# Two mixers of a hybrid encoder trunk: TensorE's queue in the order the code is written, in place of the scheduler's order

## The chip, the cores and the metric

One core of a Trainium2 chip runs the whole kernel. The engines named here are TensorE (PE, matmuls; PEld is its weight load), VectorE (DVE), ScalarE (ACT), GpSimd (POOL) and SyncE (SP, which issues DMAs). Each takes its own instructions one after the other and waits on semaphores for the others. The metric is the device time of one execution in microseconds (us), lower is better.

## What is computed

A two-layer encoder over 16 meta tokens and 512 tokens (T = 528), width 1024, 8 heads, float32. Layer 0 has mixer A, sparse attention: an indexer scores all keys, each query keeps its best 128, and attention runs over those. Layer 1 has mixer B, differential attention, two softmax maps per head with one subtracted from the other. A gated ConvFFN ends each layer.

```python
# mixer A, per block of 128 queries
score = jnp.einsum('bqh,bqhs->bqs', wib, jax.nn.relu(s))   # s: index queries x index keys
_, idx = lax.top_k(jnp.where(vis[None], score, NEG_INF), k_top)
logits = jnp.einsum('bqgrd,bqkgd->bqgrk', qg, ksel) * scale + bias
o = jnp.einsum('bqgrk,bqkgd->bqgrd', jax.nn.softmax(logits), vsel)
# mixer B, per block of 128 queries
lg = jnp.einsum('bqhd,bshd->bhqs', qb, kk) * scale + bias      # once with q1,k1 and once with q2,k2
a = attn_map(q1b, k1) - lam * attn_map(q2b, k2)
o = jnp.einsum('bqhs,bshd->bqhd', a, vb)
# every layer
h = h + mixer(rms_norm(h)); h = h + conv_ffn(rms_norm(h))
```

## The kernel before

The activations lie transposed (features on partitions, the 528 tokens along the free axis) and are cut in two halves of 272 and 256 tokens. A float32 product is made from three matmuls of rounded parts, `hi`x`hi`, `hi`x`lo` and `lo`x`hi`: `lin` (L306, in the helper `mm`) is such a projection, 8 slices of the contraction by 2 halves by 3, so 48 matmuls, for one block of 128 output features. Each block of weights is loaded by SP, rounded on ACT (`hi`, L168) and its rest taken on DVE or POOL (`lo`, L176).

`mixer_a` makes index keys and queries, the index scores (`is`, L875) and the top-k on DVE (rounds of L923 and L924 in `select`), the queries of the first group (`queries_a`, its four blocks followed by the sums of squares `stq`, L681), and then attends (`attend_a`): scores `sa` (L1024, three matmuls per piece), minimum and mask on DVE (L1026), exponent on ACT, transposes `pt` (L1128), rounding `ph` on ACT and `pl` on DVE, product with the values `pv` (L1119).

`mixer_b` goes through four pairs of heads, p = 0 to 3. `project(p)` makes keys, queries (`stq` again at L681, after the squares of L1531 on ACT) and values by 6 `lin`. `attend_b` goes through 16 units, `UNITS`: pair, head of the pair, half of the queries. In a unit a chunk of keys is a step: the scores `sb` of the next unit (L1670 and L1671) with their DVE reduction (L1673) and the exponent (L1679), the `pv` (L1745) of the chunk before, then the transposes `pt` (L1759) of this chunk, `ph` (L1763, ACT) and `pl` (L1764, DVE). The two maps are combined on DVE (L1689 to L1692).

The Python code runs once and records the instructions. The order in which it records them is made by a clock that counts estimated TensorE time: `fill(us)` lets the `filler` (the projections of the next pair, or the output projection) record `lin` matmuls until so much time has been counted, `defer` records something once the clock has passed. The filler gives nothing where it is blocked:

```python
for m in range(2):
    while self.unit < 4 * (p - 1) + 2 * m and p > 0:
        yield False
    yield from self.lin(x, lambda u, m=m: evac_q(u, m))
...
for t in range(len(chunks) + 1):
    next(nxt, None)            # scores of the next unit
    self.fill(0.5 * G)
    # pv of the chunk before, pt, ph and pl of this one
    self.fill(0.5 * G)
```

A scheduler then makes each engine's queue from the recorded instructions: by its own model of time it takes, for each engine, what is ready, and goes by the recorded order among those. In a region `tc.manual_schedule(engines=...)` the named engines keep the recorded order. The main part of `ffn` (the pairs of `up_pair`) is such a region of PE, DVE and ACT in both kernels; the mixers have none before. All of PSUM's small tiles (`sa`, `sb`, `pt`, `pv`, `stq`) share four buffers, tag "one".

Of the kernel before, what the change touches and what calls it, by code (L numbers as in the profile page):

```python
# [1876 lines left out]
@with_exitstack  # L1877
def trunk_kernel(ctx, tc, aps, out):
    t = Trunk(ctx, tc, aps, out)
    t.setup()  # L1880
    t.mixer_a()
    t.ffn(0)
    t.mixer_b()
    t.ffn(1)


# [53 lines left out]
```

## Time and profile before

| | |
|---|---|
| three timed runs | 1365.03, 1370.22, 1372.44 us; median 1370.22 |
| profiled execution, its own time | 1369.62 us |
| span from its first to its last instruction | 1367.8 us |
| PE busy in the span | 1284.9 us, 94% |
| DVE, ACT, POOL busy | 1032.4, 716.7, 343.3 us |

Mixer A runs from the start to about 290 us of the span, the first `ffn` to 655, mixer B to 985, the second `ffn` to the end. Matmuls are pipelined, so that a matmul shown with 0.28 us begins 0.12 us after the one before: the distance between starts is what one costs the queue. PEclk is the share of the full TensorE clock that was granted.

### The profile page before, as it was taken

Reading aid. Unit: us, or ns where it says so; the run is one execution under the profiler, and the core shown is the slowest. Engines: PE = TensorE matmul, PEld = TensorE weight load, DVE = VectorE, ACT = ScalarE, POOL = GpSimd, SP = SyncE. Lnnn points to the kernel's source line nnn. Section 1 sums busy time; section 2 is a strip of 40 time slices with the busy share of each in tenths; the row PEclk is TensorE's granted clock in tenths of the full one; section 3 lists DMA queues with packets and bytes.
Section 4 is the critical chain, followed back from the end, with each engine's and each line's share of the span. In section 5 each row is a group of like instructions: output and inputs, shape, how many; then the busy total and the mean of one; then the engine's idle time right before and its main releaser. Section 6 shows DMA issues by size and latency. Waiting matters only on the chain.

```text
span 1367.8 us, 25126 instructions
## 1 busy us (share of the span) xinstructions
PE 1284.9 (94%) x9688; PEld 1233.5 (90%) x9688; DVE 1032.4 (75%) x2030; ACT 716.7 (52%) x1426; POOL 343.3 (25%) x398
## 2 busy tenths in 40 slices
PE   5999889897999999989899999989897999999998
PEld 4999889897999999989799999989787999999986
DVE  6499977687888888776657777776787888888873
ACT  4453555564555555554435555655464555555541
POOL 3513543410111111103444644444510111111100
PEclk9999999989999999999899989999999999999999
DMA  7312222121455445533222222212221454554432
GB/s 236 107 61 76 88 83 80 62 78 62 117 133 146 127 125 130 132 79 106 92 63 89 68 67 63 71 48 73 67 88 62 120 146 129 127 148 127 118 90 93
DMA packets 58519, 136.03 MB, mean 99 GB/s; under 512 B 7216, under 2 KB 16736, under 8 KB 58400
## 3 DMA queue, kind: packets, MB, share of 16 engines
q1 hardware_dynamic: 48432, 114.57, 25.7%
q0 software_dynamic: 9968, 19.87, 9.5%
q8 instruction: 76, 1.25, 0.4%
q14 instruction: 43, 0.35, 0.1%
HBM read 112.46 MB, written 4.91 MB: 86 GB/s over the span
## 4 chain that ended last, share of the span: by engine, by line
PE 80%; DVE 11%; ACT 4%; issue 2%; POOL 1%; DMA 1%; SPq 0%; ACTq 0%; DVEq 0%; POOLq 0%
PE lin L306 22%; PE dn L1374 18%; PE g L1240 17%; PE v L1240 12%; DVE c L1331 2%; PE pv L1745 1%; PE stq L681 1%; PE pv L1119 1%; PE linh L306 1%; DVE lo L176 1%; DVE xl L630 1%; ACT hi L168 1%; PE sa L1024 1%; PE stk L671 1%; PE sb L1671 1%
## 5 line engine op out<-in xcount | busy, mean ns | idle before, releaser
L306 PE MATMUL lin<-xh,hi 128*128 128x256 f32 (+3 forms) x928 | 272.2, 298 | 13.6 <-DVE ht L547 7.1
L306 PE MATMUL lin<-xl,hi 128*128 128x256 f32 (+3 forms) x928 | 272.3, 295 | 2.1 <-DVE xl L630 1.8
L306 PE MATMUL lin<-xh,lo 128*128 128x256 f32 (+3 forms) x928 | 271.8, 294 | 0.0
L168 ACT CAST hi<-raw 128x512 fp32r<-128x512 f32 (+3 forms) x225 | 178.8, 824 | 90.9 <-PE lin L306 47.6
L176 DVE TENSOR_TENSOR lo<-raw,hi 128x1024 fp32r<-128x1024 f32 (+3 forms) x196 | 179.1, 929 | 55.1 <-ACT hi L168 52.1
L1410 POOL DMA_DIRECT2D ht<-y x64 | 55.8, 872 | 569.3 <-ACT y L1409 560.6
L306 PEld LDWEIGHTS lin<-xh,hi 128*128 128x128 f32 (+1 forms) x928 | 179.7, 196 | 17.1 <-ACT xh L656 8.6
L306 PEld LDWEIGHTS lin<-xl,hi 128*128 128x128 f32 (+1 forms) x928 | 181.2, 195 | 3.8 <-DVE xl L630 3.2
L306 PEld LDWEIGHTS lin<-xh,lo 128*128 128x128 f32 (+1 forms) x928 | 181.1, 195 | 0.0
L1240 PE MATMUL g<-xh,hi 128*128 128x264 f32 (+1 forms) x480 | 137.3, 286 | 11.3 <-DVE c L1331 6.6
L1374 PE MATMUL dn<-al,hi 128*128 128x256 f32 (+2 forms) x528 | 143.0, 321 | 0.0
L1374 PE MATMUL dn<-ah,lo 128*128 128x256 f32 (+2 forms) x528 | 142.2, 320 | 0.0
L1374 PE MATMUL dn<-ah,hi 128*128 128x256 f32 (+2 forms) x528 | 142.2, 321 | 0.0
L1240 PE MATMUL v<-Th,lo 128*128 128x264 f32 (+1 forms) x480 | 136.9, 285 | 0.0
L1240 PE MATMUL v<-Tl,hi 128*128 128x264 f32 (+1 forms) x480 | 136.5, 284 | 0.0
L1240 PE MATMUL v<-Th,hi 128*128 128x264 f32 (+1 forms) x480 | 136.3, 284 | 0.0
L1240 PE MATMUL g<-xh,lo 128*128 128x264 f32 (+1 forms) x480 | 136.0, 283 | 0.0
L1240 PE MATMUL g<-xl,hi 128*128 128x264 f32 (+1 forms) x480 | 135.7, 283 | 0.0
L1240 PEld LDWEIGHTS g<-xh,hi 128*128 128x128 f32 x480 | 90.4, 188 | 15.4 <-ACT hi L168 7.7
L176 DVE TENSOR_TENSOR lo<-S,hi 128x1024 fp32r<-128x1024 f32 x80 | 97.2, 1216 | 0.0
L1374 PEld LDWEIGHTS dn<-ah,lo 128*128 128x128 f32 x528 | 89.0, 188 | 7.4
L1374 PEld LDWEIGHTS dn<-ah,hi 128*128 128x128 f32 x528 | 88.8, 188 | 5.7 <-ACT hi L168 1.1
(301 smaller groups left out, 3290.7 us busy)
## 6 DMA issues: line engine op xcount, KB each, us to landing
raw<-w_up SPq DMA_DIRECT2D x88, 512.0 KB, 3.7
raw<-w_down SPq DMA_DIRECT2D x64, 256.0 KB, 3.5
ht<-y POOLq DMA_DIRECT2D x32, 264.0 KB, 3.9
raw<-w_in SPq DMA_DIRECT2D x16, 512.0 KB, 3.6
raw<-w_kv SPq DMA_DIRECT2D x16, 512.0 KB, 3.6
ht<-y POOLq DMA_DIRECT2D x32, 256.0 KB, 3.8
raw<-w_down SPq DMA_DIRECT2D x16, 384.0 KB, 3.2
nb<-nbias SPq DMA_DIRECT2D x16, 264.0 KB, 2.7
```

The lines of the kernel that those rows point to most:

```text
L168: nc.scalar.copy(hi[:, :n, :m], src)
L176: eng.tensor_tensor(lt[:, :n, :m], src, hi[:, :n, :m].bitcast(F32), op=OP.subtract)
L306: i = self.nc.tensor.matmul(o, w[wi][:, kw + k, :m], x[s][xi][:, kx + k, c0:HN[s]], start=(first and p == 0), stop=(last and p == 2))
L630: i = eng.tensor_tensor(xl[:, m, o:o + n], xfs[m][:, :n], xh[:, m, o:o + n].bitcast(F32), op=OP.subtract)
L671: self.nc.tensor.matmul(st[:88, 2 * c:2 * c + 2], sq[:, 88 * c:88 * (c + 1)], rhs, start=True, stop=True)
L681: self.nc.tensor.matmul(st[:, c:c + 2], sq[:, c0:c0 + 128], rhs, start=True, stop=True)
L1024: nc.tensor.matmul(s, q[:, c0:c0 + 128], k[:, k0:k1], start=(p == 0), stop=(p == 2))
L1119: nc.tensor.matmul(pv[:, :4 * nq], v[:, c, :], pp[:, :, :nq], start=(ci == 0 and p == 0), stop=(ci == nch - 1 and p == 2))
L1240: nc.tensor.matmul(out, w[wi][:, wk + k, :], xs[xi][:, xk + k, c0:c0 + N], start=(first and k == 0 and p == 0), stop=(k == 3 and p == 2), ...
L1331: nc.vector.scalar_tensor_tensor(t[:, z:n], u[:, off + t0 + z - d:off + T - d], w, t[:, z:n], op0=OP.mult, op1=OP.add)
L1374: nc.tensor.matmul(part(t, c0, c1, o), w[wi][:, k, :], acts[f][ai][:, c0:c1], start=(first and p == 0), stop=(last and p == 2))
L1410: nc.gpsimd.dma_start(self.h[m][:, t0:T], y[:, :n], accum_op=OP.add)
```

## The change

`mixer_a` and `mixer_b` are put in regions in which PE keeps the recorded order. No instruction is added, removed or altered, and the queues of the other engines are still made by the scheduler, which now has a given PE order to go by.

```diff
     t.setup()
-    t.mixer_a()
+    with tc.manual_schedule(engines={mybir.EngineType.PE}):
+        t.mixer_a()
     t.ffn(0)
-    t.mixer_b()
+    with tc.manual_schedule(engines={mybir.EngineType.PE}):
+        t.mixer_b()
     t.ffn(1)
```

PE's queue where mixer A's attention begins, behind the last `stq` of the first group's queries. Before:

```order
L681 MATMUL stq<-ones,sq 128x2 x5
L1024 MATMUL sa<-kh,qh 128x272
L1024 MATMUL sa<-kl,qh 128x272
L1024 MATMUL sa<-kh,ql 128x272
L1024 MATMUL sa<-kh,qh 128x256
L1024 MATMUL sa<-kl,qh 128x256
L1024 MATMUL sa<-kh,ql 128x256
L1024 MATMUL sa<-kh,qh 128x272
L1024 MATMUL sa<-kl,qh 128x272
L1024 MATMUL sa<-kh,ql 128x272
```

And of the change:

```order
L681 MATMUL stq<-ones,sq 128x2 x5
L1024 MATMUL sa<-kh,qh 128x272
L1024 MATMUL sa<-kl,qh 128x272
L1024 MATMUL sa<-kh,ql 128x272
L1024 MATMUL sa<-kh,qh 128x256
L1024 MATMUL sa<-kl,qh 128x256
L1024 MATMUL sa<-kh,ql 128x256
```

Before, one more piece of scores follows, then 13 `lin`, the fourth piece, and 60 `lin` ahead of the fifth; of the change 12 `lin`, the third and fourth piece, and 12 `lin` ahead of the fifth. So between the `stq` and the fifth piece there stand 12 matmuls of scores in both, with 73 `lin` before and 24 of the change.

PE's queue in mixer B at the first `stq` of pair 1, in the last steps of pair 0's first unit (names as above; `few` is a tile of the meta queries). Before:

```order
L681 MATMUL stq<-ind,sq 128x2 x5
L306 MATMUL lin<-xh_8145,lo 128x272
L306 MATMUL lin<-xh_7979,hi 128x256
L306 MATMUL lin<-xl_7980,hi 128x256
L306 MATMUL lin<-xh_7979,lo 128x256
L306 MATMUL lin<-xh_8145,hi 128x272
L306 MATMUL lin<-xl_8146,hi 128x272
L1745 MATMUL pv<-ph,vh 128x256
L306 MATMUL lin<-xh_8145,lo 128x272
```

And of the change:

```order
L681 MATMUL stq<-ind,sq 128x2 x5
L1745 MATMUL pv<-ph,vh 128x128
L1745 MATMUL pv<-pl,vh 128x128
L1745 MATMUL pv<-ph,vl 128x128
L1670 MATMUL sb<-kst,qst 128x272
L1671 MATMUL sb<-kl_8072,qst 128x272
L1670 MATMUL sb<-kst,qst 128x256
L1671 MATMUL sb<-kl_8072,qst 128x256
L1759 MATMUL pt<-ident,xs 128x128
L1759 MATMUL pt<-ident,few_8699 128x128
L1759 MATMUL pt<-ident,xs 128x128
```

Of the change no `lin` stands from the `stq` on for 33 rows, up to the scores `sb` that follow the fourth `pv` behind it; in the order before 82 `lin` matmuls stand among the same instructions.

DVE's queue of the change at that place; the row of `rq` reads the `stq` above, the third `pl` belongs to the first `pv` of 128x272 that follows:

```order
L176 TENSOR_TENSOR lo<-raw,hi 128x1024
L1532 SCALAR_TENSOR_TENSOR qst<-lin,gs,qst 64x528
L1764 TENSOR_TENSOR pl<-pt,ph 128x128
L1532 SCALAR_TENSOR_TENSOR qst<-lin,gs,qst 64x528
L688 TENSOR_SCALAR rq<-stq 128x8
L689 TENSOR_SCALAR rq<-stq 16x2
L1673 ISA xx,sm<-sb,tm,rq 128x272
L1673 ISA sm 128x1
L1673 ISA xx,sm<-sb,tm,sm,rq 128x256
L1673 ISA sm 128x1
L1764 TENSOR_TENSOR pl<-pt,ph 128x272
```

There follow the reductions of one more 272, one 256 and two 400 wide pieces, a `pl` of 256, one combination of 528 columns and a `pl` of 128. Before, these rows stand in nearly the same sequence (the second `qst` behind the rows of `rq`), with the keys of pair 1 (L1556, L1563) and another `lo` between the reductions; of the change those have moved behind them.

## Rows read from the trace of the kernel before

**Rows 1.** The page's head: span, then PE's busy time and the granted clock in 40 slices.

```profile
span 1367.8 us, 25126 instructions
PE 1284.9 (94%) x9688; PEld 1233.5 (90%) x9688; DVE 1032.4 (75%) x2030; ACT 716.7 (52%) x1426; POOL 343.3 (25%) x398
PEclk9999999989999999999899989999999999999999
```

**Rows 2.** Busy time by stretch: mixer A, first ffn, mixer B, second ffn.

```profile
core 0: us, PE busy (x) PEld busy (x) DVE busy (x) ACT busy (x) POOL busy (x), PEclk, DMA share, GB/s
10.00:290.00 280.00, 259.54 (x1939) 246.10 (x1940) 216.77 (x553) 138.63 (x313) 106.99 (x112) 0.97 0.30 92
290.00:655.00 365.00, 351.36 (x2846) 348.41 (x2844) 289.16 (x409) 198.70 (x348) 42.68 (x42) 1.00 0.43 113
655.00:985.00 330.00, 311.41 (x2444) 303.59 (x2444) 228.00 (x634) 176.91 (x437) 154.67 (x187) 0.94 0.23 69
```

**Rows 3.** PE's waits, mixer A then B: engine line waited for, us, times, longest.

```profile
PE pv L1119 <- ACT ph L1132: 3.0, 5, 0.7
PE pt L1128 <- POOL xx L1042: 1.8, 3, 1.0
...
PE pv L1745 <- DVE pl L1764: 3.0, 2, 1.7
PE Rk L703 <- POOL ex L698: 2.4, 2, 2.0
```

**Rows 4.** The chain that ended last, a `lin` of 48 matmuls at full clock: start, us.

```profile
113.80 5.96 PE lin L306 x48
```

**Rows 5.** Timeline of ACT before the last `stq` of mixer A: start, us.

```profile
121.99 1.05 ACT L168 CAST hi<-raw 128x1024 fp32r<-128x1024 f32 x1 [4.82 <-PE lin L306]
123.54 0.60 ACT L945 ACTIVATE sq<-lin 128x528 f32<-128x528 f32 x1
```

**Rows 6.** Timelines at mixer A's first scores: PE, DVE, POOL.

```profile
126.56 1.17 PE L681 MATMUL stq<-ones,sq 128*128 128x2 f32 x10
138.05 0.28 PE L1024 MATMUL sa<-kh,qh 128*128 128x272 f32 x1
131.02 0.19 DVE L478 TENSOR_TENSOR rq<-rq 128x40 f32<-128x40 f32 x1
136.50 0.49 DVE L1026 CUSTOM_DVE_ANT_0 xx<-sa,tm,rq 128x272 f32<-128x272 f32 x1
131.24 2.40 POOL L176 TENSOR_TENSOR lo<-raw,hi 128x1024 fp32r<-128x1024 f32 x1 [5.70 <-ACT hi L168]
133.60 3.09 POOL L1003 TENSOR_TENSOR tm<-tm,W 128x528 f32<-128x528 f32 x2
```

**Rows 7.** `lin` alone in mixer B, from pair 1's `stq` on: busy us (count).

```profile
747.20:764.90 17.70, 12.02 (x82) 10.83 (x82) 1.00 0.28 88
```

**Rows 8.** DVE groups, 700 to 950 us: shapes, count, busy us, mean ns, idle before.

```profile
L176 DVE TENSOR_TENSOR lo<-raw,hi 128x1024 fp32r<-128x1024 f32 x17 | 22.0, 1296 | 8.3 <-ACT hi L168 8.2
L1764 DVE TENSOR_TENSOR pl<-pt,ph 128x256 fp32r<-128x256 f32 x39 | 15.9, 413 | 4.6 <-ACT ph L1763 4.4
L1673 DVE CUSTOM_DVE_ANT_0 xx<-sb,tm,rq 128x400 f32<-128x400 f32 x16 | 10.0, 629 | 2.6 <-PE sb L1671 1.9 <-POOL tm L1639 0.5
L1532 DVE SCALAR_TENSOR_TENSOR qst<-lin,gs,qst 64x528 fp32r<-64x528 f32 x12 | 9.2, 766 | 2.7 <-ACT sq L1531 2.4
L1673 DVE CUSTOM_DVE_ANT_0 xx<-sb,tm,sm 128x256 f32<-128x256 f32 x16 | 8.7, 541 | 6.1 <-PE sb L1671 5.3
L1673 DVE CUSTOM_DVE_ANT_0 xx<-sb,tm,rq 128x272 f32<-128x272 f32 x16 | 8.0, 498 | 7.6 <-PE sb L1671 7.5
L1692 DVE SCALAR_TENSOR_TENSOR xx<-xx,sm 128x528 f32<-128x528 f32 x8 | 6.4, 800 | 0.1
```

**Rows 9.** ACT groups, 700 to 950 us, columns as in rows 8.

```profile
L168 ACT CAST hi<-raw 128x1024 fp32r<-128x1024 f32 x17 | 17.7, 1040 | 6.6 <-PE lin L306 6.6
L1763 ACT CAST ph<-pt 128x256 fp32r<-128x256 f32 x39 | 13.8, 362 | 5.8 <-PE pt L1759 5.1 <-PE pv L1745 0.4
```

**Rows 10.** Mixer B where the clock falls: two stretches as in rows 2, PE's timeline between.

```profile
800.00:805.00 5.00, 4.64 (x39) 4.36 (x37) 3.99 (x13) 3.74 (x10) 3.31 (x3) 1.00 0.07 15
805.00:810.00 5.00, 4.07 (x23) 4.10 (x24) 3.04 (x8) 1.89 (x5) 1.54 (x1) 0.54 0.33 107
805.93 1.89 PE L671 MATMUL stk<-ind,sq 128*88 128x2 f32 x12 [1.17 <-DVE ss L1792]
```

## The prediction

> **What bounds the kernel now.** I read the page's head first: PE is busy 94% of the span, the next engine, DVE, 75% [rows 1]. So PE decides, and a change of its order can gain what PE waits, or lose what it will wait. By stretch [rows 2], PE is busy 259.5 of 280 us in mixer A and 311.4 of 330 in mixer B: 20.5 and 18.6 us idle. The two `ffn` keep their order. The granted clock is 0.97 in mixer A and 0.94 in mixer B against 1.00 in the first `ffn`; 0.06 of 330 us is 20 us that mixer B loses to the lower level, 0.03 of 280 us is 8 us in A. The waits of PE inside attention are short [rows 3]: in A 3.0 us at `pv` and 1.8 at `pt`, in B 3.0 us at `pv`, in 2 places, of 64 steps, and 2.4 at `Rk`. So the scheduler's order leaves little to gain there; most of the idle time in both mixers stands at the norms, where there is no other work in either order.
>
> **What the change does.** No instruction is added. What changes is which PE instruction stands behind which, so the cost is time in which the first of the queue isn't ready and a `lin` that could have run stands behind it. I counted, for every `pv`, how many `lin` stand ahead of it in either order. Before, more stand ahead at each: the scheduler runs projections early while attention is held up. This lead goes up and down: in mixer A 0 to 84, down to 14, 72, 37, 89, 57, 83, and 0 at the end; in mixer B 0 to 162, then 74, 108, 84, 150, 88, 107, 84, 118, 26, 48, 22, 96, and 0. Where it rises, the order before has cover that the change lacks; where it falls, the change has the `lin` that was used before. One `lin` matmul costs 5.96/48 = 0.124 us at full clock [rows 4]. The rises are 84+58+52+26 = 220 in A and 162+34+66+19+34+22+74 = 411 in B, together 631, or 78 us. That is the upper bound: it holds if attention goes on as slowly as before and all the cover was needed. It was not, since PE found the operands of `pv` waiting for it in almost every step. The lower bound is nothing, where an operand arrives within the cover that is left. So I work out the places where the recorded order has little or no cover.
>
> **Start of attention in A.** Between the last `stq` and the fifth piece of scores lies a chain that doesn't depend on `lin`: `stq` from 126.56 to 127.73, the roots done at 131.2, bias and mask on ACT and POOL, the reduction on DVE from 136.50 to 136.99, which frees a buffer for the fifth piece (it ran at 138.05, behind `lin`) [rows 6]. That is 9.3 us behind the `stq`. Before, 12 matmuls of scores and 73 `lin` filled it; of the change 12 and 24 do: 36 x 0.124 = 4.5 us. The wait is 4.8 us. From below, POOL's `lo` of 2.40 us stands in the way of the mask [rows 6], and without it the wait is 2.4. I take 4.8, since the top-k on DVE and that `lo` stay. The `stq` itself stands right behind the projection whose squares it sums. Its squares end at 123.54+0.60 = 124.14, the rounding set off by that projection's end starts at 121.99 [rows 5]: 2.2 us, which before lay behind `lin`. From there on the recorded order spreads the `lin` more evenly over A's attention than the scheduler did, which had used them up, and I give back 3 us of the 4.8 us of waits at `pv` and `pt` [rows 3]. Mixer A: 4.8+2.2-3 = +4.
>
> **Stretches without `lin` in B.** Four times, once a pair, the filler is blocked at the queries of the next pair, and the recorded order has attention alone: 33 rows behind pair 1's first `stq`, 25 and 25 in the next two pairs and 81 in the last, `pv` among them. At the first of them, PE's own work from the `stq` to the fourth `pv` is 29 matmuls and the `stq`: 29 x 0.124 + 1.17 = 4.8 us, with an `stq` as in mixer A [rows 4, 6]. DVE must in that time do what the order shows, in its order: `lo` 1.30, two `qst` 1.53, two `pl` 0.83, two reductions of 272, two of 256 and two of 400 columns 1.00+1.08+1.26, a combination 0.80 [rows 8]: 7.8 us, without two `pl` and six small instructions. It can't begin with `lo` before ACT has made `hi`, 1.04 us [rows 9]. So the stretch lasts at least 7.8+1.0 = 8.8 us, and PE waits 4.0; with the small instructions nearer 5. I take 4.5. Before, at the same instructions, PE did 82 `lin` in 17.7 us, 12.0 us busy [rows 7], and DVE and ACT had that much more time. The stretches of pairs 2 and 3 begin with the same `lo` and `qst` and have fewer matmuls, the last has more but also more DVE work; I price each at 4.5, 4, 4 and 4.5, together 17. From both sides: 0 to 2 us each if DVE comes there with its queue empty and ACT's rounding is early; 10 us for the first if it costs the whole of the 82 `lin` (82 x 0.124 = 10.2).
>
> **The other steps of B.** About 48 steps have 12 `lin` between `pt` and `pv`, 1.5 us, against ACT's `ph` 0.36 and DVE's `pl` 0.41 [rows 8, 9]: hidden, as long as DVE takes the `pl` within 0.7 us. It has other work for 228 of 330 us [rows 2], and a `lo` or a 400-column reduction ahead costs more than that. I put 0.06 us on each, an estimate, +3, and take nothing off for B's present waits, which are mostly the norms'. Other engines get new orders too; what they shift counts only through these waits. The DMA share is 0.23 to 0.30 in the mixers [rows 2], so weights are not late.
>
> **The clock.** [...] I take the sum of the two as nothing, and 8 us either way as the bound (20 us lost in B now, 40% of it).
>
> The sum, against the profiled execution's own 1369.62 us (0.6 under the median of the three): 1369.6 + 4 + 17 + 3 = 1393.6, so **1394 us**, 1.7% slower.
>
> **The rivals.**
> - Faster: DVE and ACT keep up. It is decided at the step between `pt` and `pv`: if the chain is done within the 1.5 us of cover everywhere, and DVE arrives at the four stretches with nothing queued, the waits of rows 3 go (10.2 us) and only the lower bounds stand against it: 2.4 in A, nothing in B: 1369.6-10.2+2.4 = 1362. For it: PE waited at `pv` in 2 places of B only. Against it: that was with the cover of 20 us in front. Chance 0.14.
> - No change to be told (within 0.5%, 6.9 us, which is about what a measurement of this kernel can tell): the waits at the stretches are those that now stand elsewhere, some 5 us net: 1370 to 1376. For it: the same matmuls, and the idle time at the norms stays. Chance 0.14.
> - Much slower: the cover is needed for most of its length, because four PSUM buffers and DVE's queue hold each other up in the fixed order (a score waits for the reduction of the piece before, and all else of PE behind it), and PE's gaps bring the clock down more often. Two thirds of the 78 us: 1369.6+52 = 1422, and with 8 us of lower clock 1430. Against it: DVE has a third of its time free in B. Chance 0.14. [...]
> - My forecast, 1380 to 1412: 0.58.
>
> **How the numbers follow.** Slower by over 0.5%: 0.58+0.14 = 0.72; same 0.14; faster 0.14. The range leaves out half of the faster case and half of the much slower one, and a little of the forecast's ends: 1364 to 1424.
>
> **What would show it.** Right: PE's busy time in the mixers nearly the same as in rows 2, the idle time near 40 us in B and 25 in A; new waits of PE at `pv` on `pl`, of `sb` on the reduction, of the first `sa` on DVE; the two `ffn` unchanged to 1 us. Wrong in the first step: no wait of 3 us or more ahead of the fifth piece of scores in A. Wrong in the second: the four stretches pass with under 2 us of waits each, which would mean that DVE had done `lo` and `qst` before. Wrong altogether: DVE's queue, made for a PE that stands still, is so much better that attention goes faster than before.

## The result: slower by 8.5%, and the profile after

The changed kernel takes 1487.4 us (median of 4, 1483.5 to 1490.3), the kernel before 1371.3 us on the same chip: a ratio of 1.085, 95% interval 1.080 to 1.090. The forecast was 1394, its range ended at 1424. The direction was right; the loss is 116 us where 24 were worked out.

The head of the page of the changed kernel, to be laid beside [rows 1]:

```profile
span 1482.6 us, 25160 instructions
PE 1340.4 (90%) x9688; PEld 1277.1 (86%) x9688; DVE 1032.4 (70%) x2030; ACT 722.8 (49%) x1426; POOL 335.3 (23%) x398
PEclk9999979999999999998987879878999999999999
```

The span is 114.8 us longer with the same number of matmuls. PE's busy time has risen by 55.5 us, and what it isn't busy by 59.3 (1482.6 - 1340.4 = 142.2, before 1367.8 - 1284.9 = 82.9). So the loss has two halves, waiting and busy time that has become longer. The clock's row tells why the second: in mixer B eight of the ten slices from the 19th on hold a 7 or an 8. Busy time by stretch (us of the stretch, busy us and count of each engine, granted clock), with the three stretches of [rows 2], shifted:

```profile
core 0: us, PE busy (x) PEld busy (x) DVE busy (x) ACT busy (x) POOL busy (x), PEclk, DMA share, GB/s
10.00:317.50 307.50, 273.46 (x1938) 255.27 (x1939) 223.39 (x553) 140.67 (x313) 106.31 (x112) 0.93 0.28 84
317.50:681.50 364.00, 350.00 (x2847) 347.05 (x2846) 290.16 (x409) 199.17 (x348) 42.42 (x42) 1.00 0.43 114
681.50:1100.00 418.50, 353.77 (x2444) 339.18 (x2444) 220.73 (x633) 179.12 (x434) 149.08 (x188) 0.85 0.18 55
```

Mixer B is 88.5 us longer, mixer A 27.5, the `ffn` is not. DVE and ACT do nearly the same work in mixer B as before and are busy for 221 and 179 of 418.5 us: neither is the bound by its work. The granted clock of mixer B is 0.85 against 0.94: 0.15 x 418.5 = 63 us lost to the lower level, before 20.

PE's waits in mixer A, then in mixer B (engine, line, waited for: us in total, times, longest), to be laid beside [rows 3]:

```profile
PE pt L1128 <- POOL xx L1042: 6.3, 3, 4.9
PE pv L1119 <- DVE pl L1133: 4.9, 11, 1.1
PE sa L1024 <- DVE sm L1026: 3.7, 1, 3.7
PE stq L681 <- ACT sq L945: 3.5, 2, 2.1
...
PE stq L681 <- ACT sq L1531: 23.1, 8, 4.1
PE sb L1670 <- DVE sm L1673: 10.8, 16, 2.2
PE vt L713 <- ACT vf L1571: 8.1, 7, 2.2
PE stq L681 <- ACT sqo L1788: 4.3, 2, 2.1
PE pv L1745 <- DVE pl L1764: 2.6, 4, 1.1
```

In mixer B the most is waited at `stq`, for ACT's square of the projection that has just ended, then at `sb` for the reduction that frees a score's buffer, and at `vt` (transposes of the values) for ACT's copy of them. The next view, PE's timeline at the first `stq` of pair 1 (start, us; in brackets the wait and who ended it), is one of the four stretches that the prediction priced:

```profile
781.60 0.27 PE L1759 MATMUL pt<-ident,xx 128*128 128x128 f32 x1
785.54 2.29 PE L681 MATMUL stq<-ind,sq 128*128 128x2 f32 x10 [3.67 <-ACT sq L1531]
787.69 0.45 PE L1745 MATMUL pv<-ph,vh 128*128 128x128 f32 x1
...
788.71 0.43 PE L1671 MATMUL sb<-kl,qst 128*128 128x272 f32 x1
788.93 0.41 PE L1670 MATMUL sb<-kst,qst 128*128 128x256 f32 x1
...
795.03 0.38 PE L1745 MATMUL pv<-pl,vh 128*128 128x256 f32 x1 [1.07 <-DVE pl L1764]
...
796.06 0.33 PE L1745 MATMUL pv<-ph,vh 128*128 128x128 f32 x1 [0.41 <-ACT ph L1763]
...
797.24 0.43 PE L306 MATMUL lin<-xh,hi 128*128 128x272 f32 x1
```

PE stands for 3.67 us ahead of the `stq`. Behind it the sums take 2.29 us where [rows 6] have 1.17 for the same ten, and two neighbours of 256 to 272 columns are 0.22 us apart (788.71 and 788.93) where [rows 4] give 0.124. The stretches say the same, with the granted clock as the third column from the end:

```profile
783.50:793.70 10.20, 8.16 (x34) 7.78 (x34) 4.81 (x15) 3.98 (x9) 3.09 (x3) 0.50 0.17 52
793.70:797.20 3.50, 2.02 (x12) 1.42 (x12) 3.33 (x12) 2.00 (x6) 1.33 (x4) 0.99 0.49 134
797.20:800.60 3.40, 3.40 (x18) 3.40 (x16) 1.32 (x6) 1.54 (x6) 0.77 (x2) 0.50 0.17 47
```

Within the wait of 3.67 us a stretch of 10.2 us at a granted clock of 0.50 begins; the two waits of 1.07 and 0.41 are followed by another of 3.4 us. What held ACT's square up stands on the timelines of DVE and ACT (in the third row ACT's second copy `qst` has waited for DVE's first, which stood behind a weight's `lo`):

```profile
782.12 1.23 DVE L176 TENSOR_TENSOR lo<-raw,hi 128x1024 fp32r<-128x1024 f32 x1 [0.92 <-ACT hi L168]
783.37 0.76 DVE L1532 SCALAR_TENSOR_TENSOR qst<-lin,gs,qst 64x528 fp32r<-64x528 f32 x1
784.17 0.70 ACT L1529 ACTIVATE qst<-lin,gs 64x528 fp32r<-64x528 f32 x1 [1.34 <-DVE qst L1532]
784.88 0.61 ACT L1531 ACTIVATE sq<-lin 128x528 f32<-128x528 f32 x1
```

The table below is worked out from the traces in the same way for every run that follows, but for e6 and e16, which are told in their sections. Mixer A is the time up to the first `T` of the first `ffn`, mixer B that from the end of its last `dn` to the first `T` of the second (`T` is an `ffn`'s first product, `dn` its last). "Waits" is what of it no TensorE instruction covers, "low" the sum of the clock's records at half of full speed. A mixer's length is taken as its work at full clock, its waits, and half of its low time; so reckoned, mixer B's work is 308.1 us before and 306.9 changed, and mixer A's 250.1 and 252.0.

| run | time, us | ratio to before (95%) | A: us, waits, low | B: us, waits, low |
|---|---|---|---|---|
| before | 1371.3 | | 288.4, 29.8, 17 | 351.1, 22.5, 41 |
| changed | 1487.4 | 1.085 (1.080 to 1.090) | 315.9, 43.4, 41 | 439.8, 67.9, 130 |
| e1 region on A alone | 1395.0 | 1.019 (1.017 to 1.022) | 316.5, 43.2, 44 | 350.4, 19.7, 48 |
| e2 region on B alone | 1453.1 | 1.063 (1.059 to 1.067) | 286.3, 28.2, 14 | 439.4, 67.2, 130 |
| e3 sums later | 1476.4 | 1.079 (1.075 to 1.083) | 314.9, 44.3, 38 | 426.8, 59.1, 109 |
| e4 PE busy ahead of `stq` | 1480.7 | 1.082 (1.079 to 1.085) | 315.8, 43.4, 41 | 430.3, 54.4, 92 |
| e5 only `lin` free | 1461.7 | 1.067 (1.061 to 1.072) | 314.9, 38.1, 48 | 415.4, 45.8, 130 |
| e7 square first | 1470.3 | 1.075 (1.071 to 1.079) | 316.5, 43.1, 44 | 429.4, 58.8, 126 |
| e8 DVE and ACT fixed too | 1588.2 | 1.161 (1.157 to 1.164) | 368.0, 80.2, 82 | 495.9, 101.5, 181 |
| e9 all chained | 1487.2 | 1.084 (1.080 to 1.088) | 317.1, 43.4, 44 | 443.4, 65.3, 143 |
| e10 only sums free | 1456.9 | 1.063 (1.059 to 1.067) | 310.1, 38.7, 44 | 419.7, 52.5, 120 |
| e11 only attention free | 1428.3 | 1.042 (1.038 to 1.047) | 299.2, 35.0, 27 | 394.6, 43.2, 79 |
| e12 attention alone chained | 1447.2 | 1.056 (1.053 to 1.059) | 320.4, 38.2, 65 | 398.3, 39.6, 102 |
| e13 only `pv` free | 1454.3 | 1.060 (1.056 to 1.063) | 304.0, 37.8, 38 | 421.9, 59.0, 102 |
| e14 as e12 without `pv` | 1388.7 | 1.012 (1.009 to 1.016) | 294.6, 29.2, 31 | 366.0, 24.1, 68 |
| e15 `pv` a step later | 1474.7 | 1.074 (1.070 to 1.078) | 304.0, 40.8, 34 | 441.3, 71.8, 123 |
| e17 three edits | 1456.1 | 1.064 (1.062 to 1.066) | 304.1, 40.7, 34 | 422.5, 54.8, 123 |
| e18 three edits in before | 1372.0 | 1.003 (1.002 to 1.004) | 285.1, 26.7, 14 | 355.7, 24.6, 51 |

The ratios are to runs of before beside each, whose medians lie from 1368.7 to 1371.3. From before to the change the waits rise by 13.6 + 45.4 = 59 us, half of the low time by 12 + 44 = 56: that is the loss.

### The profile page after: what moved, and what is told of

It is laid out like the page before. It is cut to its first block, busy times and chain, and to the rows that moved or that the text cites. A ratio compares the mean times of both kernels' runs of the same rounds, so it can differ in the third digit from the quotient of the medians.

```text
span 1482.6 us, 25160 instructions
## 1 busy us (share of the span) xinstructions
PE 1340.4 (90%) x9688; PEld 1277.1 (86%) x9688; DVE 1032.4 (70%) x2030; ACT 722.8 (49%) x1426; POOL 335.3 (23%) x398
## 4 chain that ended last, share of the span: by engine, by line
PE 77%; DVE 13%; ACT 6%; issue 3%; POOL 1%; DMA 1%; SPq 0%; DVEq 0%; ACTq 0%; POOLq 0%
PE lin L306 21%; PE dn L1374 16%; PE g L1240 15%; PE v L1240 11%; PE stq L681 2%; PE pv L1745 2%; DVE c L1331 2%; ACT hi L168 2%; PE pv L1119 1%; DVE lo L176 1%; PE pt L1759 1%; PE sb L1670 1%; PE linh L306 1%; PE sb L1671 1%; DVE pl L1133 1%
## 5 line engine op out<-in xcount | busy, mean ns | idle before, releaser
L306 PE MATMUL lin<-xh,hi 128*128 128x256 f32 (+3 forms) x928 | 292.0, 316 | 7.6 <-ACT xh L656 3.6
L306 PE MATMUL lin<-xl,hi 128*128 128x256 f32 (+3 forms) x928 | 279.6, 301 | 3.9 <-DVE xl L630 3.8
L306 PE MATMUL lin<-xh,lo 128*128 128x256 f32 (+3 forms) x928 | 278.2, 300 | 0.0
L306 PEld LDWEIGHTS lin<-xh,hi 128*128 128x128 f32 (+1 forms) x928 | 190.3, 206 | 10.0 <-ACT xh L656 4.2
L306 PEld LDWEIGHTS lin<-xl,hi 128*128 128x128 f32 (+1 forms) x928 | 190.5, 205 | 5.4 <-DVE xl L630 5.3
L306 PEld LDWEIGHTS lin<-xh,lo 128*128 128x128 f32 (+1 forms) x928 | 189.9, 205 | 0.0
L1374 PE MATMUL dn<-ah,lo 128*128 128x256 f32 (+2 forms) x528 | 142.2, 320 | 0.0
```

Of the source, the lines that this page charges most:

```text
L306: i = self.nc.tensor.matmul(o, w[wi][:, kw + k, :m], x[s][xi][:, kx + k, c0:HN[s]], start=(first and p == 0), stop=(last and p == 2))
L1374: nc.tensor.matmul(part(t, c0, c1, o), w[wi][:, k, :], acts[f][ai][:, c0:c1], start=(first and p == 0), stop=(last and p == 2))
```

## The experiments

### Which mixer

```
-    with tc.manual_schedule(engines={PE}):      e1: of mixer_b taken out
-        t.mixer_b()                             e2: of mixer_a taken out
+    t.mixer_b()
```

> Only mixer A is in the region of fixed order; mixer B is left to the scheduler. In the changed kernel's profile mixer A is 27 us longer than before: 14 us more waiting and 14 us more busy time at the lower clock. Theory (each mixer's loss is its own, from its own waits): 1371 + 27 = 1398 us, mixer A 299 us long, mixer B 345 us as before. Rival (the losses feed each other, for instance by weights that come later): clearly off that sum, under 1385 or over 1410.

> Only mixer B is in the region of fixed order. Theory (own loss): 1371 + 89 = 1460 us, of it 45 us waiting and about 42 us of busy time at the lower clock, with the waits of stq on ACT's squares near 23 us as in the changed kernel. Rival (the losses feed each other): more than 8 us off 1460.

1395.0 and 1453.1: 25.5 and 83.7 us, together 109 of 116. Each mixer loses on its own account; the other one keeps the length that it has before.

### Is it the place of the small sums?

e3, and with the order of TensorE unchanged e7:

```
-            self.defer(0.895, lambda: stats_k(m, sq))        e3
+            self.defer(3.0, lambda: stats_k(m, sq))
-            self.defer(1.62, lambda: stats_q(m, sq))
+            self.defer(5.0, lambda: stats_q(m, sq))
-            self.defer(0.536, lambda: self.values(...))
+            self.defer(3.0, lambda: self.values(...))

+            nc.scalar.activation(sq, src, AF.Square)         e7: ahead of the loop
             for e in range(2):
...
-                if e == 1:
-                    nc.scalar.activation(sq, src, AF.Square)
```

> The changed kernel with the small sums of mixer B written later into the recorded order: the query sums stand 5.0 us of PE work behind their projection (1.62 before), the key sums 3.0 (0.895), the transposes of the values 3.0 (0.536). Theory (in fixed order each small instruction waits out the evacuation that feeds it, and the clock falls behind each such wait): of the 33 us of waits at stq on squares, at vt and at stk some 28 go, and of the 117 us at half clock in mixer B 50 go, worth 25 us: 1487 - 53 = 1434 us, 1420 to 1450. Rival (attention with too little cover is what holds PE, and these waits only show it): the waits move to pv, sb and pt, 1475 us or more.

> The changed kernel with ACT's square of mixer B's queries written ahead of the two copies of the same projection instead of behind them; TensorE's order stays. Theory (TensorE's waits hang on evacuations through ACT and DVE with too little cover, so a wait removed at one place comes back in part at the next): the waits of stq on squares fall from 23 to 8 to 14 us, mixer B's idle time by 3 to 7 us only, 1475 to 1484 us. Rival (each wait is a cost of its own): idle time falls with the stq waits, by 10 us or more, and the clock with it: 1460 to 1472 us.

e3 is a miss of the theory, in the rival's range: 1476.4, 11 us gained. The waits at `stq` fell from 27.3 to 5.5 us, but those at `pv` rose from 5.2 to 13.2, at `Rk` (transposes that spread the keys' factors) from 1.0 to 5.6 and at `pt` from 1.1 to 4.7, so that mixer B's waits are only 8.8 us less. e7's waits lie nearer the theory, its time in the rival's range: all waits at `stq` fell from 27.3 to 8.0, all waits of B by 9.1 (3 to 7 were expected), the time by 17 to 1470.3. Its profiled execution was its slowest, 1476.5, 8 us under the changed kernel's 1484.6, so that of the 17 us the trace shows only half. Of the waits, half or more of what is taken away at the place where PE waits comes back at the next.

### Does a wait cost the clock?

e4 fills the waits of the changed kernel, e6 makes waits in the kernel before, where there is nothing else but dense work:

```
+        for _ in range(keep):                                e4: keep = 20, ahead of mixer B's stq
+            xw = self.xb[1][0]
+            self.nc.tensor.matmul(st[:, 256:512], xw[:, 0, 0:128], xw[:, 1, 0:256], start=True, stop=True)

+                k = f % 5                                    e6: ahead of each pair of the ffn
+                nc.tensor.matmul(g[:, 0:2], self.ident, self.gap[:, 0:2], start=True, stop=True)
+                for _ in range(max(k, 1)):
+                    z = self.gap[:, :528 if k else 16]
+                    nc.gpsimd.tensor_scalar(z, z, 1.0, 1.0, op0=OP.mult, op1=OP.mult)
+                nc.tensor.matmul(g[:, 0:2], self.ident, self.gap[:, 0:2], start=True, stop=True)
```

> The changed kernel with 20 matmuls of 256 columns, whose results nobody reads, right ahead of each of mixer B's eight query sums: 8 x 20 x 0.11 = 18 us of added TensorE work, all of it where TensorE waits 1.6 to 4.1 us today. The order and every dependency stay. Theory (the lower clock follows from TensorE standing still there): the half-clock time in mixer B falls from 117 us to 60 to 80, the busy time without the added work by 18 to 28, and the time to 1459 to 1470 us. Rival (the lower clock follows from the small sums themselves, or is given regardless): half-clock time near 117 us, 1487 to 1500 us.

> The kernel before, with one wait added at each of the 40 projection pairs of the two ffn, in the middle of dense work at full clock: TensorE issues a matmul of 2 columns, GpSimd rewrites the tile that it read (one short or one to four long instructions), and TensorE reads it again. From GpSimd's rows of before (0.34 us for 16 columns, 0.74 for 528) the waits should be about 0.6, 1.0, 1.8, 2.5 and 3.3 us, eight of each, together 74 us, and the 80 small matmuls 17 us: 1371 + 91 = 1462 us if a wait costs its own length alone. Theory (a wait of 1.8 us or more costs the clock behind it as well): the half-clock time of the two ffn rises from 10 us to 130 to 190 us, worth 60 to 90 us: 1522 to 1552 us. Rival (the clock falls in the mixers because of the small sums and transposes there, not because of a wait): half-clock time under 40 us, 1462 to 1480 us.

e6 took 1505.5 us, 135 more than before: 70 us more of waits, 14 of small matmuls, and 51 of clock (the low time of the two `ffn` went from 10 to 113 us, half of the rise is 51). The theory's mechanism is there, smaller than expected (130 to 190); the rival, 1480 or less, falls. PE's timeline at one of the longest waits, and the stretches around it:

```profile
536.62 0.40 PE L1382 MATMUL dn<-ah,lo 128*128 128x256 f32 x2
536.86 0.28 PE L1263 MATMUL g<-gap,ident 128*128 128x2 f32 x2
541.24 0.58 PE L1267 MATMUL g<-gap,ident 128*128 128x2 f32 x2 [4.10 <-POOL gap L1266]
541.68 0.57 PE L1242 MATMUL g<-xh,hi 128*128 128x264 f32 x1
```

```profile
527.00:537.00 10.00, 10.00 (x85) 10.00 (x83) 8.06 (x11) 6.63 (x11) 0.89 (x1) 1.00 0.46 107
...
541.20:546.80 5.60, 5.56 (x25) 5.57 (x26) 1.62 (x3) 0.91 (x2) 0.00 (x0) 0.50 0.51 147
546.80:556.00 9.20, 9.20 (x78) 9.20 (x77) 5.62 (x9) 3.51 (x7) 0.89 (x1) 1.00 0.26 39
```

Ahead of the wait there are 10 us of dense work at 1.00, behind it 5.6 us at 0.50 with 25 matmuls where 47 fit (at the 78 in 9.2 us of the next stretch), and then 1.00 again. The 40 waits, eight of each kind, with the low time that begins behind them:

| GpSimd's work | mean wait, us | followed by low clock | mean low time, us | price of the wait, us |
|---|---|---|---|---|
| 16 columns | 0.42 | 0 of 8 | 0 | 0.4 |
| one of 528 | 0.92 | 2 of 8 | 0.9 | 1.4 |
| two | 1.45 | 4 of 8 | 1.7 | 2.3 |
| three | 2.95 | 8 of 8 | 4.3 | 5.1 |
| four | 4.06 | 8 of 8 | 7.2 | 7.7 |

The last column is the wait and half of the low time. So the waits of 2.95 and 4.06 us cost 1.7 and 1.9 times their length. The small matmuls at each wait are the same in all five kinds, so that it is the wait that makes the difference. Of the second kind the two that were followed by low clock are the longest, 1.17 and 1.18 us; the other six took 0.84 or 0.85. e4 shows the other side: with PE kept busy ahead of the eight `stq` the low time of mixer B falls from 130 to 92 us, by 38 where the expectation, which counted 117 for the changed kernel, had 37 to 57. So standing still there is a cause of the lower clock, and not the sums alone. The waits at `stq` fall by 18 us, but all of B's by 13.5 only, since `Rk` waits 5 us more, and B's work, as in the table, rises by 23 us. In time it gains 7, not 17 to 28.

### What does the order of the other two engines do?

```
-    with tc.manual_schedule(engines={mybir.EngineType.PE}):
+    with tc.manual_schedule(engines=ENGINES):                e8: PE, DVE and ACT, at both mixers
```

> The changed kernel with VectorE and ScalarE in the regions too, so that their recorded order holds as TensorE's does. Theory (what is missing is cover in TensorE's queue; what the other two engines do first matters little): 1475 to 1500 us. Rival (the scheduler's order for VectorE and ScalarE serves a fixed TensorE badly, long weight splits ahead of short evacuations): 1450 us or less.

1588.2: neither. Fixing DVE and ACT as well costs another 101 us. The scheduler's freedom on these two engines has kept the loss of the change at half of what the recorded order would cost on all three.

### Which part of TensorE's order?

In e5 and e9 to e14 the regions are replaced by a chain: each TensorE instruction of a chosen class is made to stand behind the one of these classes recorded ahead of it, and the rest is left to the scheduler as in the kernel before. The classes are `lin`, attention (`is`, `sa`, `sb`, `pt`, `pv`) and the sums and transposes of evacuations.

```
+            i = f(*args, **kw)                               matmul or transpose
+            if not t.fixed:                                  t.fixed: in the mixers
+                t.last = None
+            elif self.pin:                                   e9: all; e5: attention, sums; e10: lin, attention
+                if t.last is not None:                       e11: lin, sums; e12: attention
+                    t.behind(i, t.last)                      e13: all but pv; e14: attention but pv
+                t.last = i
```

> The kernel before, with every TensorE instruction of the two mixers that is not a lin chained to the one recorded ahead of it: sums, scores, transposes and pv stand in the order of the changed kernel, and only the lin stay with the scheduler. Theory (the loss comes from pinning the lin, so that nothing fills a wait): 1365 to 1380 us, mixer B with 20 to 28 us of waits and at most 60 us at half clock. Rival (the recorded order of the small instructions is what waits, right behind the evacuations that feed them): most of the loss stays, 1440 us or more.

> A control for the runs beside it: the kernel before with every TensorE instruction of the two mixers, lin, attention and sums, chained to the one recorded ahead of it, in place of the regions. Theory (the order costs, not the region): within 8 us of the changed kernel, 1479 to 1495 us. Rival (the region itself adds waits): under 1460 us.

> As the control, but only lin and attention (is, sa, sb, pt, pv) are chained; sums, roots and transposes of evacuations (st, R, stk, stq, Rk, vt, wt, Ro) are left to the scheduler. Theory 1 (the small sums, pinned right behind the evacuations that feed them, cost most): 1400 us or less, with mixer B's waits at 35 us or less. Theory 2 (the order of attention's own steps, in which the scheduler pushes pv back by up to 28 places, costs most): 1450 us or more.

> As the control, but only lin and the small sums are chained, and attention is left to the scheduler. Theory 1 (the pinned sums): 1450 us or more. Theory 2 (the pinned order of attention): 1400 us or less.

> As the control, but only attention's instructions are chained among themselves; lin and sums are left to the scheduler. Theory 1 (the pinned sums): 1365 to 1395 us. Theory 2 (the pinned order of attention): near the run with lin alone left free, which took 1462 us: 1440 us or more.

The control, e9, gives 1487.2: the chain costs what the region costs, so it is the order and nothing of the region itself. Left free alone, `lin` give back 26 us (e5, a miss of the theory that the pinned `lin` are the loss), the sums 30 (e10), attention 59 (e11, between the two theories), together 115 of 116. (That they add up so closely is not a rule: attention chained alone costs more than its freeing gives back.) Attention's own instructions chained alone, with all `lin` and sums free, cost 76 (e12), in mixer A more than the whole change does (32 us for 27). That is theory 2: half to two thirds of the loss comes from the order in which attention's own instructions stand.

What that order is can be counted in the recorded programs, as what stands in TensorE's queue between a `pt` and the first `pv` that reads it, mean of mixer B's 64 steps:

```
          lin    pt    pv   scores  sums
before   16.7   0.7   1.7     2.3    2.6
changed   9.3   0     0       1.9    1.3
```

In 42 of the 64 steps of the changed kernel no instruction of attention stands between (3 before). The scheduler had put the next `pt`, scores, and the `pv` of another step there; the recorded order has `pv` follow its own `pt` with what `lin` it has. (In the table a sum counts as recorded; the traces show each as two records.)

> As the control with everything chained (1487 us), but pv is left out of the chain. Theory (pv follows its pt too closely; the scheduler puts the next pt, scores and another pv between): 1440 us or less. Rival (scores and transposes must move as well, so freeing one kind of them helps little): 1465 us or more.

> As the run with attention alone chained (1447 us), but without pv: only is, sa, sb and pt are chained among themselves. Theory (pv's distance): 1395 us or less. Rival (scores and transposes): 1430 us or more.

e14 bears the theory out: with scores and `pt` chained but `pv` free the time is 1388.7, 58 us less than with `pv` in the chain. The waits of e12 and e14 in mixer B (L245 is the line of the helper that issues them all, chained or not):

```profile
PE pv L245 <- ACT ph L1788: 6.8, 12, 0.9
PE sb L245 <- DVE sm L1698: 6.2, 10, 1.3
PE Rk L245 <- POOL ex L723: 6.2, 2, 4.3
PE pv L245 <- DVE pl L1789: 3.6, 4, 2.3
```

```profile
PE lin L245 <- DVE ht L572: 4.0, 3, 2.3
PE sb L245 <- DVE sm L1698: 3.2, 5, 1.3
PE lin L245 <- DVE xl L655: 2.5, 3, 1.1
PE Rk L245 <- POOL ex L723: 2.4, 1, 2.4
```

With `pv` free the waits for `ph` and `pl` are gone from the first places, and those at `sb` and `Rk` are about half or less. Counted in the traces as in the table above, 13.6 `lin` and nothing of `pt` and `pv` stand between in e12, with no instruction of attention in 42 steps; in e14 it is 15.5 `lin`, 0.8 `pt` and 1.8 `pv`, and 4 steps, as in the kernel before. e13 is between the two theories: `pv` freed with `lin`, sums and the rest of attention pinned gives back 33 of 116.

### Can the recorded order be mended?

```
-            for t in range(len(chunks) + 1):                 e15, in both mixers alike
+            for t in range(len(chunks) + 2):
...
-                if pend is not None:
-                    c, ph, pl, q0 = pend
+                if t >= 2:
+                    c, ph, pl, q0 = pend.pop(0)
...
-                    pend = (c, ph, pl, q0)
+                    pend.append((c, ph, pl, q0))
-    GAP_B = (1.17, 1.214, 1.19, 1.3)
+    GAP_B = (0.97, 1.01, 0.99, 1.08)
```

> The changed kernel with pv recorded one step later in both mixers, behind the next pt and its lin, in buffers as many as before; the fill of mixer B per step is reduced by 17%, since its units have one step more. Theory (pv's distance): 1455 us or less, with mixer B's waits 15 us lower and its half-clock time 30 us lower than the changed kernel's 68 and 130. Rival: 1475 us or more.

> The changed kernel with three edits together: small sums later, ACT's squares first, pv one step later. Alone they took 11, 17 and 13 us from 1487. Theory (the same latencies wait at whichever instruction stands in front, so mends overlap): 1455 to 1472 us. Rival (each is a cost of its own): 1446 us or less.

> The kernel before with the same three edits, its order left to the scheduler. Theory (the scheduler sets the order by what is ready, so the recorded order hardly counts): within 10 us of before, 1361 to 1381 us. Rival (the recorded order sets priorities that matter): more than 10 us away, in either direction.

e15 ends at 1474.7, a miss of the theory at the rival's edge: mixer A gains 12 us, mixer B nothing. In B the distance is there (16.9 `lin`, 1.2 `pt` and 2.2 `pv` stand between) and the waits at `pv` fall from 5.2 to 1.3 us, but those at `stq` are as long as ever (27.2 us) and those at `sb` longer (16.3 for 10.8). So `pv`'s distance alone mends nothing in B where all else stays in the recorded order; whether the buffers of `ph` and `pl`, left as many as before, held it up was not tried. e17, all three edits at once, gives 1456.1: 31 us of the 41 that they gave one by one, so they overlap in part, and 85 us of the loss stay. The same edits under the scheduler (e18) change the time by 0.3%: there the recorded order hardly counts.

> The kernel before with 8 matmuls of 128 columns on the identity, whose results nobody reads, behind the transposes of every norm (8 x 8 x 0.21 = 14 us of added TensorE work), where TensorE has waits of 1 to 3 us. Theory (a wait costs its clock as well, also here): the half-clock time of the span falls from 70 us to 50 or less, the added work is mostly hidden, 1360 to 1368 us. Rival (the norms' waits end on other engines, and the added work comes on top): 1372 to 1384 us.

```
+            for _ in range(8):                               e16: in the norm, behind the transposes
+                i = nc.tensor.matmul(R[:, 384:512], self.ident, self.ident, start=True, stop=True)
```

This try for a faster kernel than before took 1380.7, a ratio of 1.007 (1.005 to 1.010): the low time of the span stayed at 68 us, and the added work came on top. No run beats the kernel before.

## Why the prediction was wrong

**The count of the cover.** The step that failed first is "I counted, for every `pv`, how many `lin` stand ahead of it". It took `lin` for the only cover and attention's own order for unchanged, and from that came the upper bound of 78 us. In truth the scheduler had also interleaved attention with itself; pinning attention alone costs 76 us (e12), 58 of them the place of `pv` (e14), and freeing the `lin` alone brings 26 (e5). The loss of 116 lies beyond that bound; its waits alone, 59, do not, and what takes it beyond is the clock, below.

**The start of attention in A.** The fifth piece of scores waits 3.7 us for the reduction (4.8 forecast), the last `stq` 2.1 (2.2). Both stand in the profile where they were put. Wrong was "I give back 3 us" of the waits at `pv` and `pt`: they rose, from 6.7 to 12.5 us over all of A. One `pt` alone waits 4.9 us for POOL, which had a weight split of 2.35 us and a mask ahead of it, and the low clock adds 12 us. Mixer A: +27, not +4.

**The four stretches without `lin`.** 17 us were forecast, and their waits are 5.2, 4.5, 4.5 and 6.0, together 20. The size was right, in part by luck: in the first three PE waits 3.7 to 4.1 us ahead of the `stq` for ACT's square, a wait that I had priced in A only, and behind the `stq`, where I expected it, DVE's queue costs 1.1 us in the first and nothing in the next two (0.4 us in each of the three is for ACT's `ph`). The queue that I priced is in it all the same, one step earlier: DVE's `lo` and `qst` end at 784.13, ACT's second copy begins at 784.17, and the square follows it. In the next two stretches, too, that copy begins 0.04 to 0.05 us behind DVE's `qst`, but there ACT had other work until then. From the `stq` to the fourth `pv` (785.54 to 796.06) the first stretch takes 10.5 us, not 8.8, because most of it, the 8.2 us up to 793.70, runs at a granted clock of 0.50.

**The other steps of B.** +3 was an estimate with no row behind it. The waits of mixer B rose by 45 us, 20 of them in the four stretches: the other steps cost 25. They are the `stq` outside these stretches (27.3 - 11.9 = 15 us), `vt` and `sb`. Sixteen waits at `sb`, fifteen of 0.4 to 0.7 us and one of 2.2, stand where a reduction has yet to free a score's buffer.

**The clock.** "I take the sum of the two as nothing, and 8 us either way as the bound" (a gain and a loss of clock set against each other) is the term that the sum had most wrong. No run shows either figure: the clock is worth 56 us, half of the loss and the largest error. The row for it was there: [rows 10] show what follows one wait of 1.17 us among small sums (0.54), and I priced 21 us of new waits as waits alone. At e6's prices the waits of 4.06 us in the mean cost 1.9 times their length: behind the one of 4.10 the clock is at 0.50 for 5.6 us. The lower clock follows shorter waits as well, of 1.17 us at the least in e6.

**The rivals.** "Much slower" had the mechanism, cover needed for most of its length and the clock falling with the gaps; its waits, 52 us, compare with 59 measured, its clock, 8, with 56. It had 0.14. The mark that PE's busy time stays "nearly the same as in rows 2" failed most plainly: 273.5 for 259.5, and 353.8 for 311.4. Not busy were 34.0 us in A and 64.7 in B, where 25 and 40 stood. What was forecast of the `ffn` held: 14.0 us not busy, 13.6 before.

**What stays open.** `pv` is worth 58 us where only attention is chained and 33 where all is. That it can fall back only as far as something else may run in its place would explain it, and the count between `pt` and `pv` agrees (11.2 `lin`, 0.5 `pt` and 1.2 `pv` in e13, less than in e14), but it is only argued; and e15 shows that the distance alone gains nothing in B. How much of the low time is due to many waits of some 0.5 us, and how much to the small sums themselves, wasn't separated. That the sums may have a part shows in the kernel before, where PE waits 0.27 us among 32 records of them (`stq` and `stk`) and the clock then falls:

```profile
868.00:873.70 5.70, 5.43 (x50) 1.00 0.28 82
873.70:877.10 3.40, 3.40 (x17) 0.50 0.02 7
```

## What to carry to other kernels

Before an order that a scheduler made is pinned, count what stands between each producer and its consumer over all instructions, not only over the obvious filler: here the distance from `pt` to `pv` was made of attention itself. Price every new wait of TensorE with the clock behind it: in e6's table waits of 0.92 to 4.06 us, in the middle of dense work, cost 1.5 to 1.9 times their length. Of the waits mended in a fixed order here (e3, e7) half or more came back at the next instructions, and none of the mends tried brought the time near the scheduler's: the order that goes by what is ready was the better one.

## What the runs showed of the hardware that was not expected

Short waits went before the lower clock where they came close together. In the changed kernel's mixer B two waits of 0.58 and 0.56 us at `sb`, ahead of pieces of 144 and 16 columns, are followed by 3.4 us at 0.50, with no other wait among them (3.40 - 2.26 = 1.14). The stretches (PE busy alone) and the two waits:

```profile
800.60:804.00 3.40, 2.26 (x18) 1.00 0.00 0
804.00:807.40 3.40, 3.40 (x18) 0.50 0.00 0
```

```profile
801.36 0.34 PE L1670 MATMUL sb<-kst,qst 128*128 128x144 f32 x1 [0.58 <-DVE sm L1673]
802.53 0.28 PE L1670 MATMUL sb<-kst,qst 128*128 128x16 f32 x1 [0.56 <-DVE sm L1673]
```

It is not so every time: of five such pairs of waits at `sb` that began at full clock, the clock fell to 0.50 in or behind four (at one a wait of 1.07 us stood ahead), and not behind the one at 889.6 and 890.8 us. In e6, where waits of 0.42 us stand alone in dense work, the clock never fell behind them (0 of 8).
